# A three-block model on one core: pinned transposes, whole-tile stores and late products in the RWKV element stage, a reordered group norm

## The chip, the cores and the metric

The kernel runs on one NeuronCore of one Trainium2 chip. The metric is the device time of one execution in microseconds (us): the median of 3 runs before is 3649.71 us (3649.18 to 3649.8). Engines are named as in the profile: PE is TensorE, DVE VectorE, ACT ScalarE, POOL GpSimd, SP SyncE, which issues most of the DMAs.

## The reference, cut to what matters

One sequence of 1024 tokens and 1024 channels goes through a first model of two layers and then through a second block. All is float32.

```python
# first model: layer 0 mixes by a gated linear recurrence (hawk), layer 1 by RWKV7
h = h + mix
h = h + swiglu(rms_norm(h, norm_ffn[i]), ffn_w_in[i], ffn_w_out[i])
ple = (p[i] @ ple_w_proj[i]) * sigmoid(rms_norm(h, norm_ple[i]) @ ple_w_gate[i])
h = h + ple
...
# RWKV7: per head a 64 x 64 state, one step per token
kk = k * k_k / norm;  k = k * (1.0 + (a - 1.0) * k_a)
S = S * w_t + (S a_t) b_t + v_t k_t          # a_t = -kk, b_t = kk * a
y = S r_t
yn = group_norm(y) * ln_w + ln_b
bonus = sum(r * k * r_k) * v
out = ((yn + bonus) * g) @ w_o
...
# second block: an S5 state space branch beside windowed attention, then a gate
proj = rms_norm(h) @ w_in
mixed = concat(s5(u) * silu(z_ssm), attention(q, k, v) * silu(z_attn)) @ w_out
h = h + rms_norm(mixed);  h = h + sigmoid(h @ pl_w_gate + pl_b_gate) * (p @ pl_w_proj)
```

## The kernel before

Activations lie channels on partitions, in tiles of 128 channels by 512 tokens; the 1024 tokens are two halves. Every large product is made in three fp32r matmuls (high by high, low by high, high by low: L191 to L193). One such matmul of 512 columns is called an FFN matmul below, whatever layer it is of. A weight tile comes by a DMA on SP's queue (L51), ScalarE makes its high part (L60) and VectorE its low part (L65).

Stages are generators. `both` (L1913) interleaves two of them by given numbers of steps, so that FFN matmuls stand between the instructions of a stage that has long chains of small operations. A scheduler then sets each engine's queue from its own estimate of when operands are ready; it may move an instruction ahead of others that were written earlier, if no dependence forbids it. An engine works its queue in order.

The change touches these places.

`s5_prep` (L1361) makes the matrices of the S5 branch beside the FFN of layer 0. It loads the parameters `lraw` and `draw` on POOL's queue and transposes them on TensorE (L1377, L1381).

`load_p` (L596) loads the embedding rows `pin` and transposes them (L606); `ple` (L621) multiplies them with `ple_w_proj` and gates the product. For layer 0 `ple` runs once per half of the tokens: for the first half ahead of the RWKV layer, for the second beside the recurrence of RWKV's half 0.

`rw_elem` (L849) is the element stage of RWKV: for each of eight tiles j (128 channels, two heads) the low-rank matmuls for decay and `a` (L894, L896), ScalarE's sigmoids and exponentials (L903 to L910), VectorE's products that make the tiles `AR` and `KB` (L911 to L921) with POOL's share (L918, L919, L922), the store of both to DRAM (`arD`, `kbD`), and then on TensorE the bonus (L936, from `t_r`) and the products of `KB` and `AR` (L947, into `zy`). `rw_lanes` (L969) follows, a chain of small VectorE operations that inverts triangular matrices. An FFN stage runs beside it.

`rw_b` (L997) is the recurrence: eight chunks of 64 tokens for all 16 heads, each loading its slices of `AR` and `KB`, then many matmuls of 64 x 64 (L1069, L1113, L1117, L1129, L1139, L1158) up to the new state. After every second chunk `rw_gn` (L1182) normalises `Y` of 128 tokens, adds the bonus and transposes it (L1206). FFN and `ple` matmuls run beside it.

In the second block `attn` (L1729) follows the S5 branch; its softmax chain runs on VectorE (L1763) ahead of a transpose (L1775).

Of the kernel before, what the change touches and what calls it, by code (L numbers as in the profile page):

```python
# [95 lines left out]
class Kernel:  # L96
# [80 lines left out]


# [442 lines left out]
    def ple(self, i, nin, pp, fin, halves, last=None, px=None):  # L621
        nc = self.nc
        tt = nc.vector.tensor_tensor
        if px is None:
            px = {}
            for _ in self.load_p(px, self.i["p"][i, 0], pp, halves):
                yield
        for m in range(8):
            w = self.W.get(("pg", i, m, halves))
            s = {}  # L630
            for half in halves:
# [10 lines left out]
                yield  # L642
            w = self.W.get(("pp", i, m, halves))
# [32 lines left out]
    def rw_consts(self, pool):  # L676
# [172 lines left out]
    def rw_elem(self, half, ap):  # L849
# [33 lines left out]
        v3 = lambda t: t.rearrange("p (a b) -> p a b", b=128)  # L883
        for j in range(8):
# [10 lines left out]
            for e, p in enumerate((pw, pa)):  # L895
# [19 lines left out]
            ts(out=v4(nb), in0=B, scalar1=-1.0, scalar2=self.v("rw_k_a", j), op0=ADD, op1=MUL)  # L915
            stt(out=kr, in0=nb, scalar=1.0, in1=kr, op0=ADD, op1=MUL)
# [17 lines left out]
            pb = self.psum("g")  # L934
            for q in range(4):
                nc.tensor.matmul(pb[:, 2 * q:2 * q + 2], rk[:, q * 128:(q + 1) * 128], self.hsel[:, 0, 0:2],  # L936
                                 start=True, stop=True)
# [1237 lines left out]
```

## Time and profile before

| | |
|---|---|
| median of 3 runs | 3649.71 us |
| profiled execution, its own time | 3649.47 us |
| its span | 3647.8 us (1.7 us lie outside it) |
| TensorE busy | 3372.5 us, 92% of the span |
| VectorE busy | 2382.7 us, 65% |
| granted TensorE clock, mean | 0.96 of full speed |

The span is the profiled part of one execution. Busy time is summed over an engine's instructions; its idle time lies between them. The granted clock is that of TensorE, where 1.00 is 2.4 GHz and 0.50 is 1.2 GHz; a window's number is its mean. An engine's wait is charged to what came last: the engine, the line and the tile that released it.

### The profile page before, as it was taken

Reading aid. Unit: us, or ns where it says so; the run is one execution under the profiler, and the core shown is the slowest. Engines: PE = TensorE matmul, PEld = TensorE weight load, DVE = VectorE, ACT = ScalarE, POOL = GpSimd, SP = SyncE. Lnnn points to the kernel's source line nnn. Section 1 sums busy time; section 2 is a strip of 40 time slices with the busy share of each in tenths; the row PEclk is TensorE's granted clock in tenths of the full one; section 3 lists DMA queues with packets and bytes.
Section 4 is the critical chain, followed back from the end, with each engine's and each line's share of the span. In section 5 each row is a group of like instructions: output and inputs, shape, how many; then the busy total and the mean of one; then the engine's idle time right before and its main releaser. Section 6 shows DMA issues by size and latency. Waiting matters only on the chain.

```text
span 3647.8 us, 52253 instructions
## 1 busy us (share of the span) xinstructions
PE 3372.5 (92%) x19883; PEld 2695.6 (74%) x19883; DVE 2382.7 (65%) x4118; ACT 1556.4 (43%) x2386; POOL 733.7 (20%) x1169
## 2 busy tenths in 40 slices
PE   8999699999999968998899699989999999999899
PEld 6777577777767757776678477767888888786777
DVE  8777777876566587555845884656544465677674
ACT  6656522223434442344444523433322244467553
POOL 4322358810310130011300410001000024140020
PEclk8999899999999979999999799989999999999999
DMA  3111113332533575643434756524333212231533
GB/s 100 44 50 38 37 52 93 116 115 89 162 93 117 149 184 142 162 121 100 142 122 141 169 140 165 150 81 132 96 88 97 83 59 93 83 115 36 164 98 114
DMA packets 648539, 394.79 MB, mean 108 GB/s; under 512 B 122324, under 2 KB 600320, under 8 KB 648288
## 3 DMA queue, kind: packets, MB, share of 16 engines
q1 hardware_dynamic: 640752, 377.25, 36.4%
q0 software_dynamic: 3584, 10.07, 0.8%
q10 hardware_dynamic: 3952, 4.13, 0.4%
q8 instruction: 156, 2.56, 0.3%
q14 instruction: 95, 0.78, 0.1%
HBM read 321.44 MB, written 69.93 MB: 107 GB/s over the span
## 4 chain that ended last, share of the span: by engine, by line
PE 62%; DVE 18%; DMA 8%; ACT 6%; issue 5%; SPq 1%; POOL 1%; DVEq 0%; ACTq 0%; POOLq 0%
PE mm L191 17%; PE mm L193 17%; PE mm L192 17%; DVE wlo L65 3%; DVE h L267 1%; DMA wr<-in_ffn_w_in_dram 1%; PE gg L1069 1%; DVE hgl L224 1%; DVE lnP L985 1%; DVE lnT L987 1%; PE mm L832 1%; PE mm L834 1%; PE mm L833 1%; ACT L433 1%; PE gg L1139 1%
## 5 line engine op out<-in xcount | busy, mean ns | idle before, releaser
L191 PE MATMUL mm<-hgh,whi 128*128 128x512 f32 x2272 | 909.9, 401 | 3.9 <-ACT whi L60 1.7
L193 PE MATMUL mm<-hgh,wlo 128*128 128x512 f32 x2272 | 899.9, 396 | 2.5 <-DVE wlo L65 1.8
L60 ACT CAST whi<-wr 128x1024 fp32r<-128x1024 f32 (+3 forms) x566 | 478.1, 848 | 989.0 <-PE mm L192 602.2
L192 PE MATMUL mm<-hgl,whi 128*128 128x512 f32 x2272 | 899.8, 396 | 0.0
L65 DVE TENSOR_TENSOR wlo<-wr,whi 128x1024 fp32r<-128x1024 f32 (+3 forms) x564 | 565.8, 1004 | 294.2 <-ACT whi L60 279.2
L191 PEld LDWEIGHTS mm<-hgh,whi 128*128 128x128 f32 x2272 | 434.2, 191 | 101.9 <-issue 7.5
L193 PEld LDWEIGHTS mm<-hgh,wlo 128*128 128x128 f32 x2272 | 432.8, 190 | 98.5 <-DVE wlo L65 3.9
L192 PEld LDWEIGHTS mm<-hgl,whi 128*128 128x128 f32 x2272 | 433.7, 191 | 91.8 <-issue 3.3
L191 PE MATMUL mm<-mh,whi 128*128 128x512 f32 x704 | 282.5, 409 | 30.8 <-ACT whi L60 19.2
L193 PE MATMUL mm<-mh,wlo 128*128 128x512 f32 x704 | 277.9, 402 | 13.7 <-DVE wlo L65 12.9
L192 PE MATMUL mm<-ml,whi 128*128 128x512 f32 x704 | 282.5, 402 | 1.9 <-DVE ml L197 1.9
L238 POOL TENSOR_TENSOR acc<-acc,sq 128x512 f32<-128x512 f32 x84 | 129.6, 1543 | 760.0 <-PE mm L192 385.5
L570 DVE TENSOR_TENSOR f<-mm,rstd 128x512 f32<-128x512 f32 x176 | 120.4, 686 | 247.6 <-PE mm L193 247.2
L267 DVE TENSOR_TENSOR h<-mm,h 128x512 f32<-128x512 f32 x272 | 181.7, 682 | 81.1 <-PE mm L193 80.8
L191 PEld LDWEIGHTS mm<-mh,whi 128*128 128x128 f32 x704 | 136.4, 194 | 69.4 <-ACT whi L60 22.6
L193 PEld LDWEIGHTS mm<-mh,wlo 128*128 128x128 f32 x704 | 135.7, 193 | 50.2 <-DVE wlo L65 21.3
L192 PEld LDWEIGHTS mm<-ml,whi 128*128 128x128 f32 x704 | 136.7, 194 | 31.6 <-DVE ml L197 4.3
L196 ACT CAST mh<-f 128x512 fp32r<-128x512 f32 x88 | 54.7, 621 | 211.9 <-DVE f L575 211.8
L907 POOL TENSOR_TENSOR t_s<-t_c,t_s 128x512 f32<-128x512 f32 x16 | 23.2, 1450 | 525.4 <-DVE t_c L905 525.4
L191 PE MATMUL mm<-xh,whi 128*128 128x512 f32 (+2 forms) x320 | 123.8, 398 | 4.0 <-DVE h L267 2.7
L193 PE MATMUL mm<-xh,wlo 128*128 128x512 f32 (+2 forms) x320 | 127.0, 399 | 0.4 <-DVE wlo L65 0.3
L192 PE MATMUL mm<-xl,whi 128*128 128x512 f32 (+2 forms) x320 | 127.3, 400 | 0.0
(621 smaller groups left out, 6041.6 us busy)
## 6 DMA issues: line engine op xcount, KB each, us to landing
wr<-in_ffn_w_in_dram SPq DMA_DIRECT2D x162, 512.0 KB, 3.9
wr<-in_ffn_w_out_dram SPq DMA_DIRECT2D x120, 256.0 KB, 2.7
wr<-in_rw_w_rkv_dram SPq DMA_DIRECT2D x48, 512.0 KB, 4.2
wr<-in_ple_w_gate_dram SPq DMA_DIRECT2D x24, 512.0 KB, 4.1
wr<-in_ffn_w_out_dram SPq DMA_DIRECT2D x56, 192.0 KB, 2.4
wr<-in_lru_w_in_dram SPq DMA_DIRECT2D x20, 512.0 KB, 3.8
wr<-in_w_in_dram SPq DMA_DIRECT2D x18, 512.0 KB, 4.1
hD<-h SPq DMA_DIRECT2D x32, 256.0 KB, 2.0
```

The source lines that it names most:

```text
L60: self.nc.scalar.copy(out=hi[s], in_=t[s])
L65: self.nc.vector.tensor_tensor(out=lo[s], in0=t[s], in1=f32(hi[s]), op=SUB)
L191: mm(ps, a, xh, start=start and k == 0, stop=False)
L192: mm(ps, a, xl, start=False, stop=False)
L193: mm(ps, b, xh, start=False, stop=stop and k == nk - 1)
L196: self.nc.scalar.copy(out=hi, in_=src)
L224: nc.vector.scalar_tensor_tensor(out=lo, in0=h, scalar=g, in1=f32(hi), op0=MUL, op1=SUB)
L238: nc.gpsimd.tensor_tensor(out=a, in0=a, in1=q, op=ADD)
L267: self.nc.vector.tensor_tensor(out=h, in0=ps, in1=h, op=ADD)
L433: act(out=s["a"], in_=s["r"], func=AF.Exp, scale=self.hc[:, j:j + 1])
L570: tt(out=t, in0=p, in1=nin["rstd"][half], op=MUL)
L832: mm(p[:, 0:256], xh, wh, start=k == 0, stop=False)
```

## The change

*Pins.* The transposes in `load_p`, `rw_gn` and `s5_prep` get an order edge to the TensorE instruction written before them, so that the scheduler can't move them ahead of it. *Embedding.* `ple` issues its load first and makes the transposes after the first tile's gate matmuls. *Element stage.* The bonus, the products and their stores are made one tile later than the tile itself; two VectorE operations on `kr` become one on ScalarE and one on VectorE, with a new constant `ka1`; `AR` and `KB` are stored whole, two DMAs for seven. *Recurrence.* Its loads pick their slices from the new layout, four DMAs for two. *Group norm.* POOL makes the bonus first, the multiply by `lnw` moves under the square root, and seven steps instead of four lie ahead of the last one. *S5 preparation.* Separate tiles for the parameters, their loads on SP's queue, eight steps ahead of the transposes. *Attention.* Two projection steps are put behind S5's last matmul. The step numbers of the interleaving follow (138, 43, 44). In the new function `products` the body is the removed code.

```diff
+    def pin(self, ins):
+
+        return self.tc.keep_in_program_order(ins)
...
-                    nc.tensor.transpose(p[:, q * 128:(q + 1) * 128], t[:, q, k * 128:(k + 1) * 128], self.ident)
+                    self.pin(nc.tensor.transpose(p[:, q * 128:(q + 1) * 128], t[:, q, k * 128:(k + 1) * 128], self.ident))
...
+        ld = None
-            for _ in self.load_p(px, self.i["p"][i, 0], pp, halves):
-                yield
+            ld = self.load_p(px, self.i["p"][i, 0], pp, halves)
+            next(ld)
...
+            if m == 0 and ld is not None:
+                for _ in ld:
+                    pass
...
+        self.ka1 = pool.tile([128, 8], F32, name="ka1")
+        c = self.vcol["rw_k_a"]
+        nc.vector.tensor_scalar(out=self.ka1, in0=self.vecs[:, c:c + 8], scalar1=-1.0, scalar2=1.0, op0=MUL, op1=ADD)
...
+        def products(j, AR, KB, rk):
+            pb = self.psum("g")
+            for q in range(4):
...
-            ts(out=v4(nb), in0=B, scalar1=-1.0, scalar2=self.v("rw_k_a", j), op0=ADD, op1=MUL)
-            stt(out=kr, in0=nb, scalar=1.0, in1=kr, op0=ADD, op1=MUL)
+
+            act(out=v4(nb), in_=B, func=AF.Identity, scale=self.v("rw_k_a", j), bias=self.ka1[:, j:j + 1])
+            tt(out=kr, in0=nb, in1=kr, op=MUL)
...
-            ck = lambda t: t[half].rearrange("(a e) p (j x) -> p a e j x", e=2, x=128)[:, :, :, j, :]
-            nc.sync.dma_start(out=ck(self.arD).rearrange("p a e x -> p (a e) x"),
-                              in_=AR.rearrange("p a (e b) c -> p (a e) (b c)", e=2))
-            for e in range(2):
-                r = self.hp(e)
-                nc.sync.dma_start(out=ck(self.kbD)[r, :, e, :],
-                                  in_=KB[r, :, 2 * e:2 * e + 2, :].rearrange("p a b c -> p a (b c)"))
-                for a in range(2):
-                    nc.sync.dma_start(out=ck(self.kbD)[r, :, 1 - e, a * 64:(a + 1) * 64], in_=KB[r, :, 3 - 2 * e - a, :])
-            yield
...
+            nc.sync.dma_start(out=self.arD[half][j], in_=AR.rearrange("p a b c -> p (a b c)"))
+            nc.sync.dma_start(out=self.kbD[half][j], in_=KB.rearrange("p a b c -> p (a b c)"))
+            yield
+            if late:
+                products(*late)
+                yield
+            late = (j, AR, KB, rk)
             if j == 4:
                 lane = self.rw_lanes(half, 0, ap)
             if lane is not None:
                 for _ in range(12):
                     next(lane, None)
+        products(*late)
+        yield
...
-            for nm, src in (("AR", self.arD), ("KB", self.kbD)):
-                s[nm] = bp.tile([128, 8, 128], F32, tag=nm, name=nm, bufs=2)
-                nc.sync.dma_start(out=s[nm], in_=src[half][c].rearrange("p (j x) -> p j x", x=128))
+            AR = bp.tile([128, 8, 128], F32, tag="AR", name="AR", bufs=2)
+            nc.sync.dma_start(out=AR, in_=self.arD[half][:, :, c * 128:(c + 1) * 128].rearrange("j p x -> p j x"))
+            KB, src = bp.tile([128, 8, 128], F32, tag="KB", name="KB", bufs=2), self.kbD[half]
+
+            r = self.hp(c % 2)
+            nc.sync.dma_start(out=KB[r], in_=src[:, r, c * 128:(c + 1) * 128].rearrange("j p x -> p j x"))
+            r = self.hp(1 - c % 2)
+            for a in range(2):
+                o = c * 128 + (1 - a) * 64
+                nc.sync.dma_start(out=KB[r, :, a * 64:(a + 1) * 64], in_=src[:, r, o:o + 64].rearrange("j p x -> p j x"))
+            s.update(AR=AR, KB=KB)
...
-        for _ in range(4):
+        for _ in range(7):
             yield
...
+        nc.gpsimd.tensor_tensor(out=h3(V), in0=h3(V), in1=bc(self.bonus[:, half, cp, :]), op=MUL)
...
+        tt(out=Y, in0=Y, in1=self.lnw, op=MUL)
         nc.vector.reciprocal(out=m, in_=m)
         tt(out=h3(Y), in0=h3(Y), in1=bc(m), op=MUL)
-        tt(out=Y, in0=Y, in1=self.lnw, op=MUL)
-        b = self.bonus[:, half, cp, :]
-        nc.gpsimd.tensor_tensor(out=h3(q), in0=h3(V), in1=bc(b), op=MUL)
-        tt(out=Y, in0=Y, in1=q, op=ADD)
+        tt(out=Y, in0=Y, in1=V, op=ADD)
...
-                nc.tensor.transpose(p[:, (j % 4) * 128:(j % 4 + 1) * 128], Y[:, j * 128:(j + 1) * 128], self.ident)
+                self.pin(nc.tensor.transpose(p[:, (j % 4) * 128:(j % 4 + 1) * 128], Y[:, j * 128:(j + 1) * 128],
+                                             self.ident))
...
-            raws[n] = tp.tile([16, 128], F32, name="lraw")
-            nc.gpsimd.dma_start(out=raws[n], in_=i[n][0].rearrange("(p g) n -> p (g n)", g=2))
+            raws[n] = tp.tile([16, 128], F32, name=f"lraw{n[8:]}")
+            nc.sync.dma_start(out=raws[n], in_=i[n][0].rearrange("(p g) n -> p (g n)", g=2))
...
-        nc.gpsimd.dma_start(out=draw, in_=i["ssm_d_2"][0].rearrange("(p r) -> p r", r=32))
+        nc.sync.dma_start(out=draw, in_=i["ssm_d_2"][0].rearrange("(p r) -> p r", r=32))
+        for _ in range(8):
+            yield
...
-            nc.tensor.transpose(p[:, 0:16], raw, self.ident[0:16, 0:16])
+            self.pin(nc.tensor.transpose(p[:, 0:16], raw, self.ident[0:16, 0:16]))
...
-                nc.tensor.matmul(py[:, 0:256], M[:, 2 + q, :], h[:, q, :], start=False, stop=q == 1)
+                self.s5_last = nc.tensor.matmul(py[:, 0:256], M[:, 2 + q, :], h[:, q, :], start=False, stop=q == 1)
...
-                go(both((self.ffn(0, n1, n2, mp, f0[0]), 104), (self.s5_prep(sp), 130)))
+                go(both((self.ffn(0, n1, n2, mp, f0[0]), 104), (self.s5_prep(sp), 138)))
...
-                    while n < i * 39 / 40:
+                    while n < i * 39 / 43:
...
-                    go(both((self.rw_b(1, bp), 41), (self.ffn(1, n1, n2, mp, f1[1]), 32)))
+                    go(both((self.rw_b(1, bp), 44), (self.ffn(1, n1, n2, mp, f1[1]), 32)))
...
-                for _ in range(2):
-                    next(f)
+                with self.tc.issue_after(self.s5_last.ins):
+                    for _ in range(2):
+                        next(f)
```

On TensorE's queue in the FFN of layer 0 stand, around the S5 parameters, before:

```order
L193 MATMUL mm<-hgh,wlo 128x512
L191 MATMUL mm<-hgh,whi 128x512
L192 MATMUL mm<-hgl,whi 128x512
L1377 MATMUL aux<-ident,lraw 128x16
L193 MATMUL mm<-hgh,wlo 128x512
L191 MATMUL mm<-hgh,whi 128x512
```

and after (L195 to L197 are the three matmuls of a product there, L1399 the transposes):

```order
L195 MATMUL mm<-hgh,whi 128x512
L196 MATMUL mm<-hgl,whi 128x512
L197 MATMUL mm<-hgh,wlo 128x512
L1399 MATMUL aux<-ident,lrawre_3347 128x16
L1399 MATMUL aux<-ident,lrawim_3349 128x16
L195 MATMUL mm<-hgh,whi 128x512
```

Before, 32 FFN matmuls of this stage stand ahead of the first transpose; after, 144 do, and both transposes stand together.

On TensorE's queue in the tile part of the element stage, half 0, stand before (`t_r` is the tile that the bonus matmul needs, L894 and L896 are the low-rank matmuls of the next tile):

```order
L192 MATMUL mm<-ml,whi 128x512
L193 MATMUL mm<-mh,wlo 128x512
L936 MATMUL g<-hsel,t_r 128x2 x4
L894 MATMUL g<-xw,w_11053 128x512
L894 MATMUL g<-xa,a_11054 128x512
L896 MATMUL g<-xw,w2l 128x512
L896 MATMUL g<-xa,w2l 128x512
L191 MATMUL mm<-mh,whi 128x512
```

and after (L910 is the last of 16 products of the tile one earlier, its bonus stands ahead of them; L934 and L936 are the low-rank matmuls):

```order
L910 MATMUL zy_11487<-AR,KB 64x64
L910 MATMUL zy_11488<-AR,KB 64x64
L934 MATMUL g<-xw,w_11055 128x512
L934 MATMUL g<-xa,a_11056 128x512
L936 MATMUL g<-xw,w2l 128x512
L936 MATMUL g<-xa,w2l 128x512
L196 MATMUL mm<-hgl,whi 128x512
```

Before, a tile's low-rank matmuls stand directly behind the bonus of the tile ahead of it; after, they stand behind bonus and products of the tile before that one.

On TensorE's queue near the end of the recurrence of half 0, around the embedding's transposes, stand before (L606 is those transposes, L1117 to L1158 are of a chunk of the recurrence, `hgh` and `hgl` the FFN-like matmuls of the gate):

```order
L1117 MATMUL zy_14590<-ST,G 64x64
L1129 MATMUL gg<-Z,TT 64x64 x8
L606 MATMUL mm<-ident,pin 128x128 x8
L1139 MATMUL gg<-ST,KT 64x64
L1158 MATMUL zy_14589<-ST,G 64x64 x4
L1129 MATMUL gg<-Z,TT 64x64 x8
L1139 MATMUL gg<-ST,KT 64x64 x7
L1158 MATMUL zy_14590<-ST,G 64x64 x4
L191 MATMUL mm<-hgh,whi 128x512
```

and after (L610 is the transposes, L1103 to L1149 are of the last chunk):

```order
L1103 MATMUL gg<-ident,KB 128x128 x4
L1133 MATMUL zy_15197<-S,AR 64x64
L1137 MATMUL zy_15197<-ST,G 64x64 x4
L1133 MATMUL zy_15196<-S,AR 64x64 x8
L1137 MATMUL zy_15196<-ST,G 64x64 x4
L1149 MATMUL gg<-Z,TT 64x64
L1133 MATMUL zy_15197<-S,AR 64x64 x8
L1137 MATMUL zy_15197<-ST,G 64x64 x4
L610 MATMUL mm<-ident,pin 128x128 x8
L1149 MATMUL gg<-Z,TT 64x64 x7
L195 MATMUL mm<-ph,whi 128x512
```

Before, the transposes stand about three chunks ahead of the recurrence's end; after, in its last chunk, and the last FFN-like matmul ahead of them is about 2.4 chunks away.

## Rows read from the trace of the kernel before

**Rows 1.** The page's part 1: busy time, share of the span, instructions.
```profile
span 3647.8 us, 52253 instructions
...
PE 3372.5 (92%) x19883; PEld 2695.6 (74%) x19883; DVE 2382.7 (65%) x4118; ACT 1556.4 (43%) x2386; POOL 733.7 (20%) x1169
```

**Rows 2.** Waits of TensorE by releaser: total us, times, longest.
```profile
PE gg L1206 <- DVE Y L1200: 22.5, 2, 11.4
...
PE g L936 <- DVE t_r L921: 21.1, 11, 4.4
...
PE aux L1377 <- DMA lraw<-in_ssm_lam_re_dram: 18.3, 1, 18.3
PE zy L947 <- POOL KB L918: 15.8, 2, 7.9
PE mm L1775 <- DVE sc L1763: 12.9, 2, 7.9
...
PE mm L606 <- DMA pin<-in_p_dram: 9.8, 2, 5.3
PE zy L947 <- DVE AR L914: 9.7, 5, 3.3
```

**Rows 3.** Instructions on tile `lraw`: ns min/median/max, first and last start in us.
```profile
L1377 PE MATMUL aux<-ident,lraw x2: 235/259/283, 449.3 to 459.4; 16*128 16x16 f32 x2
L1371 POOL DMA_DIRECT2D lraw<-in_ssm_lam_re_dram x1: 553/553/553, 430.3 to 430.3; - x1
```

**Rows 4.** Busy time in windows behind four long waits of TensorE, with granted clock.
```profile
core 0: us, PE busy (x) PEld busy (x) DVE busy (x) ACT busy (x) POOL busy (x), PEclk, DMA share, GB/s
449.30:461.00 11.70, 11.70 (x39) 9.17 (x40) 7.02 (x35) 1.68 (x2) 0.53 (x1) 0.73 0.05 13
921.10:930.40 9.30, 9.29 (x33) 7.76 (x34) 2.61 (x3) 2.38 (x4) 0.87 (x1) 0.70 0.37 106
1623.50:1633.50 10.00, 9.97 (x74) 8.43 (x75) 2.65 (x5) 2.27 (x5) 0.00 (x0) 0.69 0.06 15
1709.40:1720.60 11.20, 10.47 (x39) 8.44 (x40) 2.06 (x9) 2.20 (x4) 0.00 (x0) 0.74 0.63 198
```

**Rows 5.** Windows: element stage, tiles and what follows, halves 0 and 1.
```profile
1236.00:1374.00 138.00, 101.97 (x643) 77.23 (x642) 111.88 (x166) 69.93 (x90) 49.04 (x33) 0.83 0.69 170
1374.00:1458.30 84.30, 76.94 (x327) 61.89 (x327) 65.52 (x142) 21.88 (x29) 0.00 (x0) 0.98 0.58 139
1990.00:2127.70 137.70, 101.53 (x638) 77.60 (x639) 113.57 (x167) 70.00 (x90) 50.62 (x33) 0.82 0.68 165
2127.70:2212.60 84.90, 79.00 (x330) 63.11 (x328) 64.74 (x142) 21.62 (x29) 0.00 (x0) 0.96 0.59 142
```

**Rows 6.** VectorE by line, tile part of half 0: busy, mean ns, idle before.
```profile
L916 DVE SCALAR_TENSOR_TENSOR kr<-nb,kr 128x512 f32<-128x512 f32 x8 | 8.3, 1042 | 0.1
...
L267 DVE TENSOR_TENSOR h<-mm,h 128x512 f32<-128x512 f32 x8 | 5.4, 680 | 0.6 <-PE mm L193 0.6
...
L915 DVE TENSOR_SCALAR nb<-KB,vecs 128x512 f32<-128x512 f32 x8 | 3.7, 467 | 1.1 <-ACT KB L904 1.1
```

**Rows 7.** Windows: first chunk's opening, recurrence, last chunk's second part, last norm.
```profile
1455.00:1469.70 14.70, 8.08 (x170) 7.54 (x170) 3.80 (x5) 2.73 (x4) 0.00 (x0) 0.64 1.08 258
1456.00:1693.00 237.00, 218.46 (x3115) 175.99 (x3116) 134.52 (x210) 97.71 (x181) 19.36 (x13) 0.95 0.47 130
2436.20:2442.60 6.40, 5.50 (x145) 4.99 (x144) 4.54 (x9) 3.50 (x8) 0.00 (x0) 1.00 0.34 100
2442.60:2453.60 11.00, 0.06 (x1) 0.09 (x2) 9.01 (x9) 1.36 (x2) 1.90 (x1) 0.64 0.00 0
```

**Rows 8.** DMA issues: count, KB each, median us to landing.
```profile
arD<-AR SPq DMA_DIRECT2D x16, 512.0 KB, 3.7
...
kbD<-KB SPq DMA_DIRECT2D x64, 64.0 KB, 2.4
```

**Rows 9.** Timeline of the last norm of half 1: start, duration, us.
```profile
2450.85 1.22 DVE L1197 TENSOR_TENSOR Y<-Y,lnw 128x1024 f32<-128x1024 f32 x1
```

More of the change, by code (lines that the diff above doesn't have):

```diff
@@ L883, in rw_elem @@
         v3 = lambda t: t.rearrange("p (a b) -> p a b", b=128)
+        def products(j, AR, KB, rk):
+            pb = self.psum("g")
+            for q in range(4):
+                nc.tensor.matmul(pb[:, 2 * q:2 * q + 2], rk[:, q * 128:(q + 1) * 128], self.hsel[:, 0, 0:2],
+                                 start=True, stop=True)
+            nc.vector.tensor_copy(out=self.bonus[:, half, :, 2 * j:2 * j + 2],
+                                  in_=pb[:, 0:8].rearrange("p (a b) -> p a b", b=2))
+            nt = at("nt", 2)
+            pe = [self.psum("zy0"), self.psum("zy1")]
+            for ch in range(8):
+                cp, par = ch // 2, ch % 2
+                o = 64 if par == 0 else 0
+                for e in range(2):
+                    rows = slice(e * 64, e * 64 + 64)
+                    nc.tensor.matmul(pe[e][o:o + 64, cp * 64:cp * 64 + 64], KB[rows, cp, 1 + par, :],
+                                     AR[rows, cp, 1 + par, :], start=True, stop=True)
+            for e in range(2):
+                tt(out=nt[:, e * 256:(e + 1) * 256].rearrange("p (a b) -> p a b", b=64),
+                   in0=pe[e][:, 0:256].rearrange("p (a b) -> p a b", b=64),
+                   in1=self.mstrict.unsqueeze(1).to_broadcast([128, 4, 64]), op=MUL)
+            for sd in range(2):
+                par = 1 - sd
+                dst = self.ntD[half][2 * j:2 * j + 2, par:8:2].rearrange("e c s t -> s (e c) t")
+                src = nt[sd * 64:(sd + 1) * 64, :].rearrange("p (a b) -> p a b", b=64)
+                nc.sync.dma_start(out=dst, in_=src)
+                dst = self.ttD[0:32, :, 32:64].rearrange("s (je c) t -> s je c t", c=8)[:, 2 * j:2 * j + 2, par:8:2, :]
+                nc.sync.dma_start(out=dst.rearrange("s e c t -> s (e c) t"), in_=src[0:32, :, 32:64])
+        late = None
         for j in range(8):
@@ L933, in rw_elem @@
-            yield
[L934 to L937, printed above, removed]
-            nc.vector.tensor_copy(out=self.bonus[:, half, :, 2 * j:2 * j + 2],
-                                  in_=pb[:, 0:8].rearrange("p (a b) -> p a b", b=2))
-            nt = at("nt", 2)
-            pe = [self.psum("zy0"), self.psum("zy1")]
@@ L942, in rw_elem @@
-            for ch in range(8):
-                cp, par = ch // 2, ch % 2
-                o = 64 if par == 0 else 0
-                for e in range(2):
-                    rows = slice(e * 64, e * 64 + 64)
-                    nc.tensor.matmul(pe[e][o:o + 64, cp * 64:cp * 64 + 64], KB[rows, cp, 1 + par, :],
-                                     AR[rows, cp, 1 + par, :], start=True, stop=True)
-            for e in range(2):
-                tt(out=nt[:, e * 256:(e + 1) * 256].rearrange("p (a b) -> p a b", b=64),
-                   in0=pe[e][:, 0:256].rearrange("p (a b) -> p a b", b=64),
-                   in1=self.mstrict.unsqueeze(1).to_broadcast([128, 4, 64]), op=MUL)
@@ L953, in rw_elem @@
-            for sd in range(2):
-                par = 1 - sd
-                dst = self.ntD[half][2 * j:2 * j + 2, par:8:2].rearrange("e c s t -> s (e c) t")
-                src = nt[sd * 64:(sd + 1) * 64, :].rearrange("p (a b) -> p a b", b=64)
-                nc.sync.dma_start(out=dst, in_=src)
-                dst = self.ttD[0:32, :, 32:64].rearrange("s (je c) t -> s je c t", c=8)[:, 2 * j:2 * j + 2, par:8:2, :]
-                nc.sync.dma_start(out=dst.rearrange("s e c t -> s (e c) t"), in_=src[0:32, :, 32:64])
@@ L1380, in s5_prep @@
         p = self.aux()
-        nc.tensor.transpose(p[0:32, 0:16], draw, self.ident[0:16, 0:16])
+        self.pin(nc.tensor.transpose(p[0:32, 0:16], draw, self.ident[0:16, 0:16]))
         nc.vector.tensor_copy(out=dT, in_=p[0:32, 0:16])
```

## The prediction, made before the changed kernel was run

> **What bounds the kernel now.** I read the page's busy times first: TensorE works 3372.5 of 3647.8 us, VectorE 2382.7 [rows 1]. So a change can win at most TensorE's 275 us of idle time, and what its half clock costs behind that idle time. Next I read TensorE's waits by releaser [rows 2]. They aren't spread evenly. Two waits for the group norm's last result make 22.5 us, one wait for a parameter of the S5 preparation 18.3, two for the per-layer embedding (`pin`) 9.8, two for the softmax 12.9. The element stage (`rw_elem`) has many short ones: 21.1 for `t_r`, 15.8 for `KB`, 9.7 for `AR`. Third come the windows behind the long waits, for the clock: after each of them TensorE runs at 1.2 GHz for some microseconds before 2.4 GHz is granted again, so the granted share is 0.69 to 0.74 there [rows 4].
>
> The page calls TensorE the bound, but not everywhere. In the part of the element stage that works on the eight tiles, 138 us long in either half, TensorE is busy 102 us at a granted 0.83, and VectorE 112 [rows 5]. VectorE is the busier one there. An FFN matmul takes 76.94/327 = 0.235 us in the part behind the tiles [rows 5]; I use 0.23 at full clock.
>
> **The stalls that go.** TensorE works its queue in order, so one early-placed instruction whose operand is late holds everything behind it.
>
> *S5 preparation.* The load of `lraw` goes out on POOL at 430.3 and TensorE transposes it at 449.3 [rows 3]; 18.3 us of that are idle [rows 2]. In the new order the transposes stand behind 144 FFN matmuls of this stage, not 32: 112 x 0.23 = 26 us later, and the load stands on SP's queue, ahead of where the wait was. The wait should go. Behind it the clock cost 11.7 us x (1 - 0.73) = 3.2 us [rows 4]. Gain 21.5 us.
>
> *Embedding transposes.* The load now goes out before the first gate matmuls. The transposes stand behind 24 of them (5.5 us) for the first half of the tokens, and behind the last chunk of the recurrence for the second. Two waits of together 9.8 us [rows 2], and 9.3 x 0.30 + 10.0 x 0.31 = 5.9 us of clock [rows 4]: gain 15.7.
>
> *Last group norm of half 0.* In before only 13 FFN-like matmuls (3 us) stand between the last chunk and the eight transposes; after, 104 FFN and gate matmuls (24 us) stand ahead of them, more than the 11.0 us of the norm's chain [rows 7]. Gain: the half-0 share of the 22.5 us, 11.1 [rows 2], and 11.2 x 0.26 = 2.9 of clock [rows 4]: 14.0.
>
> These are 51 us. I take 50: what is late next is VectorE, which now meets some of these tiles among its other work.
>
> **The element stage.** In before, the low-rank matmuls of the next tile (L894, L896) stand behind the bonus matmul (L936) that needs `t_r`, the last VectorE result of the present tile. So the tiles go one after the other: matmul, ScalarE, VectorE, matmul. After, they stand behind the products of the tile before the present one, and two tiles can be under way. That takes the TensorE waits away, but not VectorE's work. The edit on `kr` takes a tensor_scalar (467 ns) and a fused multiply (1042 ns) away and adds a plain multiply, whose nearest row is 680 ns [rows 6]: 8 x 0.83 = 6.6 us less per half. ScalarE gets eight instructions more; it is busy 70 of 138 us [rows 5] and hides them.
>
> So the tile part can't be shorter than VectorE's work, 111.9 - 6.6 = 105 us, and need not be longer than now, 138. Nothing in the trace shows two tiles under way, so I take the middle, 121. Behind the tiles stand 409 FFN matmuls after, 327 before: 409 x 0.23 = 94, and I add 2 for lane waits. Together 217, against 138.0 + 84.3 = 222.3 before [rows 5]. But from the stage's first low-rank matmul to the recurrence there are 678 FFN matmuls after and 615 before: 63 x 0.23 = 14.5 us of work that the next stage no longer has. Gain 222.3 + 14.5 - 217 = 20 us per half, with the ends 105 + 94 (gain 38) and 138 + 94 (gain 5). Half 1 has the same windows and the same order: 40 in all, 10 to 76.
>
> The two whole-tile stores replace seven, the products' four stores stay; the chain of the stage doesn't run over SP, so I count them as nothing. If that cover is gone, five issues fewer per tile only help.
>
> **What the recurrence loses.** The FFN work taken early is missing in `rw_b`. In half 0, with the embedding's transposes pinned behind the last chunk's matmuls, its later gate matmuls can't come forward; about 2.4 chunks stand with no FFN matmul between them. The price of such a bare chunk isn't in the trace as a whole. Its second part alone takes 6.4 us; the upper end adds the 14.70 - 8.08 = 6.6 us that TensorE is idle in the first chunk's opening, where the loads come last, so 13 [rows 7]. I take the middle, 10: 24 us, of which TensorE works some 4 per chunk, so 14 are lost, and 3 at low clock behind it as after every long wait [rows 4]. Loss 17, from 8 to 24.
>
> In half 1 the last group norm still stands directly behind the last chunk, with no filler. Its wait stays; the reordering takes at most the multiply by `lnw`, 1.2 us, from its chain [rows 9]. And 1.3 chunks ahead of it become bare: 13 us with 5 of work, 3 of which were bare already. Net loss 4 (1 to 8).
>
> A ScalarE or VectorE reordering inside the norm changes nothing where other matmuls cover it: cost 0.
>
> The Trainium skill's page "TensorE: Matmul & The Clock Gate", section "Part 1: The HAM clock gate", says that throttled is the default state and that activity releases it. By it the bare chunks would run at 1.2 GHz throughout, and their 10 us of matmuls would cost 10 more: a sum of 57 and not 67. The trace is divided on it: 0.64 granted where the first chunk waits, 1.00 in a bare chunk's second part [rows 7].
>
> **Loads of the recurrence.** Two loads per chunk become four, in pieces of 512 and 256 bytes. On the store side before, 512 KB of `AR` in 512-byte pieces landed in 3.7 us, and 64 KB of `KB` in 256-byte pieces in 2.4 us [rows 8]. A chunk takes 237/8 = 30 us [rows 7] and its tiles are double-buffered, so I count 0; the price without that cover is the second rival's.
>
> **Attention.** The order of TensorE's softmax part stays; ten FFN-like matmuls (10 x 0.23) move behind S5's last one and uncover a short wait. The 12.9 us for `sc` [rows 2] stay. Loss 2 (0 to 4).
>
> **Sum.** 50 + 40 - 17 - 4 - 2 = 67 us. The profiled execution took 3649.5 us, span and 1.7 us outside it, the median of the runs 3649.7. 3649.5 - 67 = 3582.5; on the median 3583.
>
> **The rivals.**
> *VectorE holds the element stage.* Gain there 5 per half, bare chunks at their upper price: 50 + 10 - 24 - 8 - 4 = 24, so 3626. For it: VectorE is busy 112 of 138 us already [rows 5]. Against it: every tile shows a TensorE wait for `t_r` or `KB` [rows 2], which is idle time of the loop, not only of TensorE.
>
> *Slower: small pieces make the recurrence wait for its loads.* If each of the 16 chunks waits as the first one does now, 6.6 us, that is 106 us, less 67: 3689. It decides from 67/16 = 4.2 us per chunk on. For it: the DMA share is 1.08 in the first chunk's opening [rows 7]. Against it: a chunk has 30 us to load in, and TensorE is idle for only 18.5 us over all eight chunks, 6.6 of them in the first [rows 7]. The Trainium skill's page "DMA: Bandwidth & Descriptors", section "Specifications", gives 512 bytes as the least transfer for line rate; by it half of `KB` would load slower than before. The rows agree in direction: 64 KB in 2.4 us is less per microsecond than 512 KB in 3.7 [rows 8].
>
> *The element stage is filled.* It reaches VectorE's 105 us, gain 38 per half, and the bare chunks cost their lower end: 50 + 76 - 8 - 2 - 1 = 115, so 3535. For it: the waits and the low clock of this stage vanish together. Against it: VectorE would have to work without a pause.
>
> *It doesn't do what it says.* The pinned transposes wait where they now stand, or VectorE's lateness comes back as waits of other matmuls: a fifth of the 50 us lost again, no gain in the element stage, the bare chunks at the upper end: 40 - 36 = 4, so 3645. Against it: the new places are 5 to 26 us behind the old ones.
>
> **How the numbers follow.** Forecast 0.52 (its own range 3565 to 3605), VectorE 0.20, filled 0.18, slower 0.05, no change 0.05. The range 3533 to 3632 takes in the forecast and both cases on its sides up to their values, and leaves out about 0.2. What a measurement here can tell from no change is about 0.2%, 7.3 us. Faster: 0.52 + 0.20 + 0.18 = 0.90; same 0.05; slower 0.05.
>
> **What would show it.** Right: no wait of TensorE on the S5 parameters and on `pin` over 1 us, and none in the group norm of half 0; in the element stage TensorE's waits on `t_r` and `KB` largely gone, with VectorE over 85% busy and the tile part near 121 us; a stretch of 20 to 30 us near the end of the half-0 recurrence with TensorE about 40% busy. Wrong: a tile part that stays near 138 us or reaches 105, waits on the loads of `AR` and `KB` in the middle of the recurrence, or bare chunks much over 13 us each.

## The result, and the profile after

The changed kernel takes 3591.05 us (median of 4 runs, 3585.62 to 3593.05) against 3649.44 us before: a ratio of 0.9839, 95% interval 0.9822 to 0.9856, so 1.6% faster, 58 us. The forecast was 3583 with a range of 3533 to 3632. The total came out near it; several of the steps behind it didn't.

The page of the changed kernel, busy times, which answer to [rows 1]:

```profile
span 3591.3 us, 52160 instructions
...
PE 3378.7 (94%) x19883; PEld 2700.2 (75%) x19883; DVE 2369.6 (66%) x4103; ACT 1583.5 (44%) x2412; POOL 735.8 (20%) x1166
```

TensorE does the same 19883 matmuls in about the same busy time. What left the span is its idle time: 275 us before, 213 after. Where they went is read from its waits by releaser (total us, times, longest), which answer to [rows 2]:

```profile
PE mm L1797 <- DVE sc L1785: 12.9, 2, 7.9
PE mm L196 <- DVE hgl L228: 12.1, 1, 12.1
...
PE g L899 <- DVE t_r L962: 10.3, 8, 2.6
...
PE gg L1225 <- DVE Y L1219: 9.5, 1, 9.5
PE g L934 <- ACT KB L944: 9.0, 2, 4.5
PE mm L1511 <- DVE XB L1495: 8.1, 3, 5.2
```

The waits for `lraw` and `pin` are gone and of the two norm waits one is left (9.5 us, half 1, as forecast); the softmax keeps its 12.9. In the element stage 21.1 us for `t_r` became 10.3, and `KB` and `AR` from POOL and VectorE no longer appear; two waits of 4.5 us for `KB` from ScalarE are new. But a new wait of 12.1 us for `hgl` stands where that for `lraw` was.

The element stage in windows (tile part and what follows; half 0, then half 1), which answer to [rows 5]:

```profile
1229.50:1349.60 120.10, 101.56 (x623) 75.56 (x621) 100.61 (x144) 79.83 (x100) 50.32 (x33) 0.86 0.66 190
1349.60:1448.20 98.60, 95.42 (x410) 77.36 (x409) 76.48 (x166) 26.06 (x35) 0.00 (x0) 0.98 0.53 126
...
1952.50:2075.60 123.10, 99.89 (x626) 74.11 (x624) 104.84 (x145) 81.95 (x102) 50.51 (x33) 0.88 0.64 185
2075.60:2174.00 98.40, 95.59 (x415) 77.47 (x411) 77.87 (x166) 27.25 (x35) 0.00 (x0) 0.98 0.54 133
```

The columns after the length are TensorE, its weight loads, VectorE, ScalarE, POOL, granted clock, DMA share and GB/s. The tile part takes 120.1 us where 121 was forecast, and the part behind it 98.6 where 96 was.

The table cuts each run's trace at the same instructions: the first low-rank matmul of a half, its last product, the first state matmul of the recurrence, the last norm transpose. Lengths are in us, in brackets the FFN matmuls in the stretch. It is worked out from the starts of those instructions.

| | to tiles 0 | tiles 0 | behind | recurrence 0 | between | tiles 1 | behind | recurrence 1 | rest |
|---|---|---|---|---|---|---|---|---|---|
| before | 1236.2 | 137.4 (288) | 84.7 (327) | 253.6 (498) | 277.0 (804) | 138.0 | 85.6 | 243.4 | 1191.8 |
| changed | 1229.5 | 119.9 (269) | 98.8 (409) | 241.0 (459) | 263.3 (780) | 122.9 | 98.6 | 225.2 | 1192.0 |
| a1 | 1233.5 | 119.9 (269) | 97.2 (409) | 243.5 (459) | 263.7 (780) | 122.5 | 97.2 | 225.1 | 1194.3 |
| a2 | 1214.9 | 120.6 (269) | 99.1 (409) | 240.8 (459) | 264.9 (780) | 122.2 | 99.2 | 224.0 | 1196.0 |
| a4 | 1229.4 | 126.7 (312) | 95.1 (369) | 242.3 (456) | 265.4 (780) | 126.9 | 96.0 | 223.0 | 1191.9 |
| a5 | 1227.8 | 121.5 (269) | 98.9 (409) | 243.5 (459) | 267.6 (780) | 121.7 | 98.8 | 232.2 | 1194.2 |
| a6 | 1230.8 | 119.4 (269) | 97.7 (409) | 241.3 (435) | 279.7 (804) | 121.4 | 98.8 | 229.1 | 1193.8 |
| b1 | 1229.0 | 110.2 (243) | 105.7 (415) | 241.9 (479) | 265.2 (780) | 110.7 | 108.0 | 229.1 | 1192.4 |
| b2 | 1229.3 | 125.3 (231) | 101.2 (372) | 241.8 (534) | 264.8 (780) | 128.7 | 99.3 | 236.5 | 1195.2 |
| b3 | 1229.4 | 137.1 (286) | 86.0 (327) | 239.1 (524) | 263.7 (780) | 140.1 | 84.0 | 235.3 | 1191.9 |
| b5 | 1230.4 | 148.0 (377) | 85.0 (325) | 231.8 (435) | 267.4 (780) | 150.4 | 87.3 | 216.5 | 1190.8 |
| c1 | 1213.1 | 120.4 (269) | 98.7 (409) | 238.1 (459) | 265.0 (780) | 121.9 | 99.9 | 223.3 | 1192.9 |
| p1 | 1216.6 | 137.5 (288) | 83.1 (327) | 255.9 (498) | 278.7 (804) | 137.4 | 86.0 | 243.1 | 1192.6 |

Run p1 differs from the kernel before in one load of the first stretch; its other stretches differ from those of before by up to 2.3 us, so smaller differences in the table mean nothing.

### The profile page after: what moved, and what is told of

It is laid out like the page before. It is cut to its first block, busy times and chain, and to the rows that moved or that the text cites. A ratio compares the mean times of both kernels' runs of the same rounds, so it can differ in the third digit from the quotient of the medians.

```text
span 3591.3 us, 52160 instructions
## 1 busy us (share of the span) xinstructions
PE 3378.7 (94%) x19883; PEld 2700.2 (75%) x19883; DVE 2369.6 (66%) x4103; ACT 1583.5 (44%) x2412; POOL 735.8 (20%) x1166
## 4 chain that ended last, share of the span: by engine, by line
PE 65%; DVE 16%; DMA 6%; ACT 6%; issue 5%; SPq 1%; POOL 1%; DVEq 0%; ACTq 0%; POOLq 0%
PE mm L195 18%; PE mm L197 18%; PE mm L196 18%; DVE wlo L65 3%; DVE h L271 1%; DVE hgl L228 1%; DMA wr<-in_ffn_w_in_dram 1%; ACT whi L60 1%; DMA wr<-in_ffn_w_out_dram 1%; DVE lnP L997 1%; PE gg L1089 1%; PE mm L843 1%; PE zy L1133 1%; PE mm L845 1%; ACT L437 1%
## 5 line engine op out<-in xcount | busy, mean ns | idle before, releaser
L196 PE MATMUL mm<-hgl,whi 128*128 128x512 f32 x2272 | 898.1, 395 | 12.1 <-DVE hgl L228 12.1
L195 PE MATMUL mm<-hgh,whi 128*128 128x512 f32 x2272 | 904.2, 398 | 1.8 <-DVE hgl L228 0.8
L197 PE MATMUL mm<-hgh,wlo 128*128 128x512 f32 x2272 | 897.2, 395 | 2.6 <-DVE wlo L65 2.0
L195 PEld LDWEIGHTS mm<-hgh,whi 128*128 128x128 f32 x2272 | 432.2, 190 | 97.8 <-issue 5.1
L197 PEld LDWEIGHTS mm<-hgh,wlo 128*128 128x128 f32 x2272 | 431.2, 190 | 97.3 <-DVE wlo L65 4.5
L195 PE MATMUL mm<-mh,whi 128*128 128x512 f32 x704 | 283.1, 409 | 26.4 <-ACT whi L60 19.6
L197 PE MATMUL mm<-mh,wlo 128*128 128x512 f32 x704 | 281.5, 405 | 9.1 <-DVE wlo L65 8.5
L195 PEld LDWEIGHTS mm<-mh,whi 128*128 128x128 f32 x704 | 136.2, 194 | 64.9 <-ACT whi L60 26.6
L197 PEld LDWEIGHTS mm<-mh,wlo 128*128 128x128 f32 x704 | 136.6, 194 | 48.1 <-DVE wlo L65 18.5
L197 PE MATMUL mm<-xh,wlo 128*128 128x512 f32 (+2 forms) x320 | 126.3, 397 | 0.4 <-DVE wlo L65 0.3
L195 PE MATMUL mm<-xh,whi 128*128 128x512 f32 (+2 forms) x320 | 122.9, 395 | 1.3 <-ACT kt L828 1.3
```

The source lines that it names most:

```text
L195: mm(ps, a, xh, start=start and k == 0, stop=False)
L196: mm(ps, a, xl, start=False, stop=False)
L197: mm(ps, b, xh, start=False, stop=stop and k == nk - 1)
```

## The experiments

Each run is timed against the kernel before on the same chip. Differences from the changed kernel are taken from the ratios (0.9839 is 3591 on 3649.4). The interval of a ratio reaches 5 to 7 us to either side, so a difference of less than some 8 us between two runs can't be told from none.

**What became of the 21.5 us of the S5 preparation.** VectorE before, at that place (start, duration, line, and in brackets how long it was idle and for what):

```profile
434.65 1.23 DVE L65 TENSOR_TENSOR wlo<-wr,whi 128x1024 fp32r<-128x1024 f32 x1
449.09 0.17 DVE L1296 TENSOR_SCALAR ae<-st 128x16 f32<-128x16 f32 x1 [13.22 <-DMA wr<-in_ffn_w_in_dram]
449.18 0.75 DVE L224 SCALAR_TENSOR_TENSOR hgl<-h,vecs,hgh 128x512 fp32r<-128x512 f32 x1
```

and after:

```profile
439.09 1.26 DVE L65 TENSOR_TENSOR wlo<-wr,whi 128x1024 fp32r<-128x1024 f32 x1
454.06 0.17 DVE L1316 TENSOR_SCALAR ae<-st 128x16 f32<-128x16 f32 x1 [13.72 <-DMA st<-in_ssm_log_step_dram]
454.15 0.75 DVE L228 SCALAR_TENSOR_TENSOR hgl<-h,vecs,hgh 128x512 fp32r<-128x512 f32 x1
```

In both, VectorE stands for 13 us at the first use of `st`, with `hgl` behind it, which TensorE needs. Before, TensorE was held by `lraw` until 449.3 anyway, so this wait didn't show in its list. The page's releaser of 449.09 is a weight DMA; the line's operand is `st`.

Run a1 undoes the S5 edits in the changed kernel:

```diff
-            nc.sync.dma_start(out=raws[n], in_=i[n][0].rearrange("(p g) n -> p (g n)", g=2))
+            nc.gpsimd.dma_start(out=raws[n], in_=i[n][0].rearrange("(p g) n -> p (g n)", g=2))
...
-        for _ in range(8):
-            yield
...
-            self.pin(nc.tensor.transpose(p[:, 0:16], raw, self.ident[0:16, 0:16]))
+            nc.tensor.transpose(p[:, 0:16], raw, self.ident[0:16, 0:16])
```

> The changed kernel with the S5 preparation's edits undone (loads of lraw and draw on POOL's queue, no pins there, no eight steps, 130). Theory one (the step of the prediction fell: in the kernel before VectorE sat idle for 13.2 us in the same stretch for st, loaded in 4-byte pieces, with a split that TensorE needs queued behind, so the wait for lraw hid a second one of nearly the same end): within 5 us of the changed kernel, at 3588 to 3597, with the 18 us wait for lraw back and the 12 us wait for the split gone. Rival (the prediction's term holds and something else ate it elsewhere): 21 us slower, 3612.

Measured: 3601.24 us, ratio 0.9862 (0.9848 to 0.9875), 8 us slower than the changed kernel: outside the 5 us of theory one, far from the rival's 21. The wait for `lraw` is back and the 12.1 us for `hgl` are gone:

```profile
PE aux L1397 <- DMA lraw<-in_ssm_lam_re_dram: 17.2, 1, 17.2
```

So the two waits do stand for each other. What the edits are worth, some 8 us, is at the edge of what can be told from nothing; in the table 4.0 us of it lie in the stretch up to the tiles.

Run a2 loads `st` in whole rows:

```diff
-        for g in range(2):
-            nc.sync.dma_start(out=st[g * 64:(g + 1) * 64, :], in_=ls[:, g, :].to_broadcast([64, 16]))
+        stw = tp.tile([128, 32], F32, name="stw")
+        nc.sync.dma_start(out=stw, in_=i["ssm_log_step_2"].to_broadcast([128, 32]))
+        for g in range(2):
+            r = slice(g * 64, (g + 1) * 64)
+            nc.vector.tensor_copy(out=st[r, :], in_=stw[r, :].rearrange("p (a g) -> p a g", g=2)[:, :, g])
```

> The changed kernel with the log-step parameter st loaded in one DMA of 128 rows of 128 bytes and spread by two VectorE copies, in place of two DMAs of 4-byte pieces. Theory one: st lands within 5 us of its issue, VectorE goes on, the 12.1 us wait of TensorE for hgl goes and about 3 us of low clock behind it: 15 us faster than the changed kernel, 3576. Rival (the queue is held by the 64-byte pieces of br and bi, or by the weight loads, not by st): st still lands some 20 us after its issue, no difference, 3591.

Measured: 3579.79 us, ratio 0.9801 (0.9788 to 0.9815), 14 us faster than the changed kernel. In the changed kernel the DMA view gives `st` 21.4 us from issue to landing (the trace holds the landing of one of the two loads):

```profile
st<-in_ssm_log_step_dram SPq DMA_DIRECT2D x2, 4.0 KB, 21.4
```

In a2 the copies that use it run at 439.15, and the `hgl` wait of 12.1 us is gone:

```profile
439.15 1.41 DVE L1410 COPY st<-stw 64x16 f32<-64x16 f32 x2
440.60 1.41 DVE L228 SCALAR_TENSOR_TENSOR hgl<-h,vecs,hgh 128x512 fp32r<-128x512 f32 x2
```

Run a3 is a1 and a2 together.

> Both of the two runs above: the S5 preparation as in the kernel before, but st in 128-byte rows. Theory one with st as the cause of both waits: lraw lands early too, neither wait stands, 3574 to 3582, no slower than the run with st in rows alone; the pins and SP's queue are worth nothing once st is quick. Rival (lraw is late for POOL's queue's sake): the wait for lraw stays at 10 to 18 us, 3590 or more.

Measured: 3584.48 us, ratio 0.9814 (0.98 to 0.9827). The wait for `lraw` is down to 0.7 us, though POOL loads it as before. It lies 2 us above theory one's range, and its interval overlaps that of a2: with `st` quick, the pins and SP's queue can't be told from nothing. Run p1 makes a2's edit in the kernel before, and nothing else.

> The kernel before with nothing changed but st loaded in 128-byte rows. Theory one (the 4-byte pieces hold both lraw and st until 449 us, so this edit alone takes the 18.3 us wait and the clock behind it away): 15 to 21 us faster than the kernel before, 3629 to 3636. Rival (lraw is late for POOL's queue's sake): within 5 us of 3650.

Measured: 3634.26 us, ratio 0.9951 (0.9937 to 0.9966): 16 us by the medians, 18 by the ratio: the 18.3 us wait and its clock come for the most part from this one load. In the table the gain lies in the first stretch, 19.6 us in the profiled execution. `lraw` on POOL's queue (first and last start):

```profile
L1377 PE MATMUL aux<-ident,lraw x2: 230/230/230, 434.9 to 442.7; 16*128 16x16 f32 x2
L1371 POOL DMA_DIRECT2D lraw<-in_ssm_lam_re_dram x1: 556/556/556, 432.8 to 432.8; - x1
```

It is transposed 2.1 us after its issue, against 19.0 in [rows 3]. What made it late stood on another queue. How it did that isn't shown; it wasn't the bandwidth, as the kernel before in the middle of that wait shows (DMA share and GB/s are the last two columns):

```profile
430.00:447.00 17.00, 0.99 (x5) 0.48 (x3) 5.84 (x10) 3.77 (x5) 4.87 (x7) 0.65 0.09 5
```

**The element stage.** Run a4 makes the products in their tile's own step:

```diff
-            if late:
-                products(*late)
-                yield
-            late = (j, AR, KB, rk)
+            products(j, AR, KB, rk)
+            yield
```

> The changed kernel with bonus and products made in the same step as their tile, not one tile later; stores, loads, ScalarE's part of kr and all else as changed. Theory one (the later products are what lets two tiles be under way): most of the 36 us that the two element stages gave are lost, 3615 to 3630, and the waits for t_r and KB are back. Rival (the gain is from fewer stores on SP's queue and 6.6 us less on VectorE per half): at most 12 us slower, 3592 to 3603.

Measured: 3598.32 us, ratio 0.9847 (0.9833 to 0.986), which can't be told from the changed kernel. The rival's range holds it. Run b1 puts `kr` back on VectorE:

```diff
-            act(out=v4(nb), in_=B, func=AF.Identity, scale=self.v("rw_k_a", j), bias=self.ka1[:, j:j + 1])
-            tt(out=kr, in0=nb, in1=kr, op=MUL)
+            ts(out=v4(nb), in0=B, scalar1=-1.0, scalar2=self.v("rw_k_a", j), op0=ADD, op1=MUL)
+            stt(out=kr, in0=nb, scalar=1.0, in1=kr, op0=ADD, op1=MUL)
```

> The changed kernel with kr made by two VectorE operations again (tensor_scalar and fused multiply), none of it on ScalarE. On-time products cost only some 7 us, so about 29 of the element stages' 36 us come from something else. Theory two (VectorE is the bound of the tile part, so its 6.6 us per half count in full): 13 us slower, 3604. Rival (the stores are the cause): at most 4 us slower, 3591 to 3595.

Measured: 3596.81 us, ratio 0.9857 (0.9842 to 0.9872): between the two expectations, and its interval too overlaps the changed kernel's. Its tile part in half 0 is shorter than the changed kernel's, with both operations on `kr` back on VectorE (third busy time):

```profile
1229.00:1339.20 110.20, 94.76 (x587) 68.94 (x587) 97.80 (x139) 67.20 (x86) 48.88 (x31) 0.86 0.67 193
```

It holds 243 FFN matmuls for 269, and what follows is 6.9 us longer. With the new stores 243, 269 and 312 FFN matmuls in the tile part go with 110.2, 119.9 and 126.7 us (b1, the changed kernel, a4). So its length goes with how much work the scheduler puts into it, and doesn't tell by itself what the stage gains. Run b2 puts back the seven stores per tile and the two loads per chunk, as the diff of the change shows them.

> The changed kernel with the old layout: seven strided stores per tile and two loads per chunk in the recurrence; products still one tile late, kr still on ScalarE. Rival to theory two (seven stores at the head of SP's queue, six of which wait for KB, hold the weight loads behind them and free AR and KB late): 12 to 20 us slower, 3603 to 3611, with SP waiting longer on KB. Theory two: within 5 us of the changed kernel, 3586 to 3596.

Measured: 3623.81 us, ratio 0.992 (0.9908 to 0.9933), 30 us slower, more than either expected. TensorE waits 18 us at once for `t_r` in either half; in half 0:

```profile
PE g L899 <- DVE t_r L962: 21.7, 3, 18.0
```

VectorE ahead of it, and SP's queue (start and duration of issues):

```profile
1316.48 0.18 DVE L951 COPY dec<-AR 128x8 f32<-128x8 f32 x1 [1.74 <-ACT AR L948]
1322.97 0.19 DVE L1004 TENSOR_TENSOR lnP<-lnN,lnT 128x31 f32<-128x31 f32 x1 [6.32 <-DMA lnN<-ntD]
...
1326.34 0.75 DVE L962 SCALAR_TENSOR_TENSOR t_r<-rr,vecs,kr 128x512 f32<-128x512 f32 x1
```

```profile
1311.50 0.61 SPq L972 DMA_DIRECT2D kbD<-KB  x1
1312.21 0.57 SPq L920 DMA_DIRECT2D ntD<-nt  x1
...
1316.26 2.26 SPq L996 DMA_DIRECT2D lnN<-ntD  x2
```

SP issues one DMA after the other, some 0.6 us each. The lanes' load `lnN` comes late, VectorE stands at its first use, and the elementwise work behind, with `t_r` at its end, is late with it. In the kernel before, with the same stores but products on time, VectorE waits 1.6 us for `lnN`.

Run b3 undoes all three edits.

> The changed kernel with all three edits of the element stage undone together (products on time, kr on VectorE, old stores and loads). Either theory, if the gain in the element stage is this stage's own: the sum comes back, 30 to 40 us slower, 3621 to 3631. Rival (part of it is from what the pins and step numbers elsewhere move into this stage): 15 to 25 us slower, 3606 to 3616.

Measured: 3608.04 us, ratio 0.9884 (0.9871 to 0.9898), 16 us slower: the rival's range. The table says why it isn't 36, which counts in the FFN work that the two stages take over. The tile part is back at 137 us. Tile part and what follows take 223.1 us with 613 FFN matmuls in half 0, and 218.7 with 678 in the changed kernel; at 0.235 us for a matmul [rows 5] that is 20 us won, an estimate. But the recurrence of half 0 takes 239.1 us with 524 FFN matmuls in b3, and 241.0 with 459 in the changed kernel: 17 us lost, as 65 matmuls fewer (15 us) stand in it and it still takes 1.9 us longer. Half 1 gives 18 won (224.1 us with 616, 221.5 with 681) and 5 lost (235.3 with 494, 225.2 with 429). Together that is 16.

Run b5 is b2 with `KB`'s six stores on POOL's queue (`nc.gpsimd.dma_start` for `nc.sync.dma_start`).

> The run with the old stores and loads (late products, 3624), but with the six stores of KB per tile issued on POOL's queue; TensorE's queue is the same to one instruction. Theory three (SP's queue is the cost: six issues of some 0.6 us per tile stand ahead of the lanes' load and of weight loads, and VectorE waited 6.3 us for that load with t_r behind it, TensorE 18 us): SP is free, the 18 us wait goes, 3592 to 3608. Rival (the 512- and 256-byte pieces hold the DMA engines, or KB's buffers come free late): 3616 or more.

Measured: 3608.28 us, ratio 0.9878 (0.9862 to 0.9895), 15 us faster than b2 and at the upper end of theory three. The long wait in the tile part of half 0 is gone (up to 1355 us; over the whole tile part 12.4 us, the longest 6.1):

```profile
PE g L899 <- DVE t_r L962: 10.2, 3, 6.1
```

The expectation's clause that TensorE's queue is the same is wrong: the table shows 377 FFN matmuls in the tile part of half 0 against 231. So this run agrees with SP's queue as the cause, but doesn't settle it alone.

**Norm and embedding.** Run a5 takes the norm back:

```diff
-                self.pin(nc.tensor.transpose(p[:, (j % 4) * 128:(j % 4 + 1) * 128], Y[:, j * 128:(j + 1) * 128],
-                                             self.ident))
+                nc.tensor.transpose(p[:, (j % 4) * 128:(j % 4 + 1) * 128], Y[:, j * 128:(j + 1) * 128], self.ident)
...
-        for _ in range(7):
+        for _ in range(4):
```

with the old order of its operations and the old step numbers.

> The changed kernel with the group norm as before: no pins on its transposes, old order of its operations, four steps ahead of the last one, step numbers 40 and 41. The prediction's term: the wait of the last norm of half 0 is back, 11 us and 3 of clock, less what the order gives elsewhere: 10 to 16 us slower, 3601 to 3607. Rival (the wait went because of the embedding's pinned transposes, which pushed the gate matmuls behind the last chunk, not because of the norm's edits): the half-0 wait stays away, within 4 us of the changed kernel.

Measured: 3612.53 us, ratio 0.9892 (0.9879 to 0.9906), 19 us slower, over the expected range. Its norm waits are two again, one of 4.4 us in half 0 beside the 11.4 of half 1:

```profile
PE gg L1226 <- DVE Y L1220: 15.8, 2, 11.4
```

Its profiled execution is 15.0 us longer than the changed kernel's: by the table 6.8 us in the recurrence of half 0 and the stretch behind it, and 7.0 in the recurrence of half 1. So the wait of half 0 is the smaller part of it.

Run a6 takes the embedding's edits back:

```diff
-            ld = self.load_p(px, self.i["p"][i, 0], pp, halves)
-            next(ld)
+            for _ in self.load_p(px, self.i["p"][i, 0], pp, halves):
+                yield
```

without the pins in `load_p`.

> The changed kernel with the embedding's edits undone (no pins on its transposes, its load and transposes together ahead of the gate matmuls). The prediction's term: both waits for pin come back, 9.8 us and 5.9 of clock, less 2 to 4 that the present kernel waits in their place: 8 to 14 us slower, 3599 to 3605. Rival (the transposes moved back free the gate matmuls of the second half of the tokens to fill the bare chunks at the end of the half-0 recurrence): within 5 us of the changed kernel.

Measured: 3612.76 us, ratio 0.9888 (0.9872 to 0.9904), 18 us slower; neither expectation reached so far. Waits of TensorE:

```profile
PE gg L1225 <- DVE Y L1219: 19.1, 2, 9.5
...
PE mm L610 <- DMA pin<-in_p_dram: 6.1, 2, 5.4
```

Besides the wait for `pin`, the norm wait of half 0 is back with 9.6 us, with the norm's own edits in place. The pinned embedding transposes hold the gate matmuls until after the last chunk, and there they cover the norm. Of the 11.1 us of this wait the norm's edits without the embedding's take 1.5 away, the embedding's without the norm's 6.7, both together all. Of the 20.8 us by which a6's profiled execution is longer, 16.7 lie in the recurrence of half 0 and the stretch behind it. The four parts undone one by one make 8 + 18 + 19 + 16 = 61 us, the change 58; each is uncertain by some 8 us, so the sums can't show how far they overlap.

**A faster version.** Run c1 is a2, and in half 1 the last FFN steps are queued behind the last chunk's matmuls:

```diff
+            with self.tc.issue_after(self.rwb_tail.ins) if self.rwb_tail else ExitStack():
+                try:
+                    next(f)
```

> The run with st in 128-byte rows, and beside it, in the recurrence of half 1, the last FFN steps held on TensorE's queue behind the last chunk's matmuls, so that some 60 of them stand between the last chunk and the norm's transposes. Theory (the last norm's 9.5 us wait and the clock behind it can be filled, and the chunks that lose these matmuls lose less): 5 to 12 us faster than with the rows alone, 3568 to 3575. Rival (as in half 0, matmuls taken from the chunks ahead leave those bare and the wait only moves): within 4 us of 3580.

Measured: 3575.00 us (3570.47 to 3582.55), ratio 0.9795 (0.9776 to 0.9815), the fastest run. The norm's wait fell from 9.5 to 4.2 us:

```profile
PE gg L1227 <- DVE Y L1221: 4.2, 1, 4.2
```

The median is in the expected range, but the interval overlaps a2's; the step beyond a2 is 5 us by the medians, 2 by the ratios, and not shown; in the table the recurrence of half 1 is only 0.7 us shorter than in a2. Against the changed kernel c1 is some 16 us faster.

## Why the prediction was right, and where it wasn't

*S5 preparation: forecast 21.5 us, measured 8 (a1).* This step failed. "The wait should go" held, but not its gain: VectorE was held by `st` until 449.09, TensorE by `lraw` until 449.3. The prediction asked what would be late next, answered "VectorE" in a general way, and priced it at 1 us, though the timeline of before had the 13.2 us on VectorE in it. It also didn't ask why the load was late; p1 shows the 4-byte pieces of `st` to be the reason.

*Embedding and last norm: forecast 15.7 and 14.0, together 29.7.* One by one they measure 18 and 19, but not as the terms have it. The waits of half 0 went, and the cover, FFN and gate matmuls ahead of the norm's transposes, was seen rightly. But the prediction counted the two edits as independent: the waits for `pin` that a6 brings back are 6.1 us, and its larger part is the norm wait. And in a5 7.0 us are lost in the recurrence of half 1, from which the prediction took no gain but 1.2 us for the multiply. That the two numbers came out near 15.7 and 14.0 is in part luck.

*Element stage: forecast 40, less 17 and 4 in the recurrences: 19 net. Measured 16 net (b3).* The size is right, and so is the account of it, 20 won and 17 lost in half 0 by b3; the reasons are right only in part. The tile part fell to 119.9 and 122.9 us, as the middle of the bounds said, but that is partly luck: b1 has 110.2 and a4 126.7, with other numbers of FFN matmuls in it and no difference in total that can be told. Nor is VectorE's work a bound of 105 us: in b1 VectorE is busy 97.8 us there, with 15 of the lanes' operations (`lnP` and `lnT`) in the tile part for 37 before, so work can leave it. And products one tile later aren't enough: with the old stores they are 13 us slower than products on time (b2 against b3, which also has the old `kr`), and with the new stores their absence can't be measured (a4). "I count them as nothing", said of the stores, was wrong: late products with the old stores, and the old loads of the recurrence, are 30 us slower than the changed kernel (b2). That SP's queue is the way it happens is argued from b2's timeline and agrees with b5. VectorE is 84 and 85% busy in the tile parts, about the forecast 85. One reading of before was too strong: "every tile shows a TensorE wait for `t_r` or `KB`", where [rows 2] has 11 waits for `t_r` and 2 for `KB` over 16 tiles.

*Bare chunks of half 0: forecast 24 us with TensorE about 40% busy, 17 lost.* This step failed too, though its number held. In windows of the changed kernel:

```profile
1600.00:1630.00 30.00, 22.35 (x556) 18.35 (x554) 20.88 (x30) 15.41 (x29) 0.00 (x0) 0.90 0.49 108
1630.00:1660.00 30.00, 29.04 (x443) 24.43 (x444) 13.13 (x26) 11.04 (x24) 0.00 (x0) 0.87 0.15 45
```

The idle time is 7.65 + 0.96 = 8.6 us and the low clock costs 30 x 0.10 + 30 x 0.13 = 6.9: together 15.5, and 17 by b3. But the stretch with no FFN matmul is 49 us long, from 1600.5 to 1649.5, not 24: some 20 us for each of the 2.4 chunks, well over the 13 that the prediction named as a sign of being wrong. TensorE is busy for 40.4 of the 49 us (82%) with small matmuls. The prediction had priced a whole chunk from its second part, at 10 us with 4 of work. The loss came out near the forecast by two errors that cancel, a stretch twice as long and TensorE twice as busy in it. The other sum, 57 with these chunks at 1.2 GHz throughout, lies nearer to the measured 58, but not for its reason: the granted clock was 0.90 and 0.87, not 0.50. TensorE waits for `AR` and `KB` from DRAM at most 1.0 us at a time, so the loads in small pieces cost nothing that shows, as forecast. They do land later for their size: 512 KB of `KB` in 3.6 us before, 256 KB in 512-byte pieces in 4.9 us after and 128 KB in 256-byte pieces in 5.9.

*Norm of half 1: the wait stayed, 9.5 us for 11.4, as forecast.* The net loss of 4 us in that recurrence didn't come: it is 18.2 us shorter than before with 65 FFN matmuls less, which are 15 us. *Attention: forecast 2 us lost; the rest after the recurrence of half 1 is 1192.0 for 1191.8, nothing.* No run undoes this edit.

The sum: forecast 67, measured 58 (56.5 by the two profiled executions). By the table 6.7 us were won up to the tiles, where the terms of S5 preparation and of the first `pin` wait, less 1, make 28. From the tiles of half 0 to those of half 1 it is 30 us, where the forecast has 25 (20 - 17 for the stage and the recurrence, 8 for the second `pin` wait, 14 for the norm). Half 1 gives 20 for 16 and the rest 0 for a loss of 2. So 21 us are missing at the start, and the total is as near as it is because the other stretches gave some 10 more than forecast. That part is luck.

## What to carry to other kernels

When a wait is to be removed, look on the other engines' timelines for idle time that ends at the same moment: one slow transfer can hold several engines, and the list of one engine's waits shows only the last. Filling one stage with work taken from the next is worth only what the next stage doesn't need it for; count both. Edits that look independent can need each other (late products and few stores, pinned transposes in two places), so undo them one by one and all together.

## What the runs showed of the hardware that wasn't expected

A load of 4 KB in 4-byte pieces on SP's queue took 14.1 us to land in the kernel before and 21.4 us in the changed one (of two such loads the trace holds one landing). In the kernel before, an 8 KB load on POOL's queue issued 4 us behind them took 19.0 us, though the DMA engines were 9% busy from 430 to 447 us; with the 4-byte pieces gone it took 2.1 us (p1). SP took 7.5 us to issue the two loads of `br` behind them, and 1.4 us in p1. SP issues a store of `KB` or of the products in some 0.6 us, so that ten of them per tile take some 6 us of the 15.7 us that a tile of b2 has (125.3/8).
